# Two recurrence inverses in one pair of PSUM banks, chain products kept together, low-rank lo weights at full height

## The chip, the cores and the metric

The kernel runs on one core of a Trainium2 chip. The time is the device time of one execution in microseconds (us). A core has five engines with a queue of instructions each: TensorE (PE), which multiplies; VectorE (DVE), ScalarE (ACT) and GpSimd (POOL), which work on elements; and SyncE (SP), which issues most DMAs. Each engine takes its own instructions in order; between engines semaphores tell when data are ready. TensorE writes to PSUM, which has eight banks; a tile of 128 x 512 float32 fills one.

## The reference

One encoder layer is applied to two groups of rows (1024 and 256), 1280 in all, of width 1024. Cut to what matters here:

```python
x = x + 0.5 * rms_norm(swiglu(rms_norm(x), ...))       # first FFN
p_rw, p_att, p_gate = split(rms_norm(x) @ w_in)
y_a = rwkv7_bidir(p_rw, ...)                           # the recurrence
y_b = axial_gqa(p_att, ...)                            # attention
x = x + rms_norm((sig(gA) * (y_a @ w_branch_a) + sig(gB) * (y_b @ w_branch_b)) @ w_out)
x = x + 0.5 * rms_norm(swiglu(rms_norm(x), ...))       # second FFN

def _rwkv7_step(S, inp):                               # in rwkv7_bidir, per head and direction
    r, w, k, v, kk, b = inp
    sa = einsum('ij,j->i', S, -kk)
    S = S * w[None, :] + sa[:, None] * b[None, :] + v[:, None] * k[None, :]
    return S, einsum('ij,j->i', S, r)
```

w and a (from which k and b are made) come out of two low-rank products, `tanh(wd) @ w_up` and `ad @ a_up`, of rank 64 for each of two directions.

## The kernel before

The program is traced instruction by instruction and then scheduled: every engine's order is fixed before the run by priority, which follows the order of the trace, and by readiness. So the code's loops give the order of the work only roughly.

**Prep.** `columns` runs the big projections (L165, in `projT`) and between them, in pieces, `prep`, 20 times (4 pairs of heads q, 5 blocks of 256 rows). A piece begins with the low-rank products: for each direction d and each of w and a, one product of the weights' high half (L576, all 128 rows of the array: both directions' rows stand in `hi`, and the activations of the other direction are its low part) and one of the low half `lo` (L577), which has 64 rows, those of the direction. ACT takes tanh out of PSUM (L578), POOL scales (L580), DVE scans and multiplies (L597 to L616), and the results go to DRAM. A copy `go` of the gate product (L585) is stored by a DMA (L586). All tiles come from pools of buffers by tag; a tile that takes a buffer waits until that buffer's last reader is done.

**Recurrence.** `run` goes through 80 steps: for each q, 20 chunks of 64 rows, the forward and the backward direction of two heads together. A step has three parts. `front` (L676 to L696) multiplies a chunk's keys and queries (g), transposes, and writes Bm and Bl, the matrix that has to be inverted, high and low half in float16. `inv` (L709 to L733) inverts it: a start on POOL and DVE (L709, L711), five levels of two matmuls (L715), a mask on DVE (L717), four matmuls (L720, L721) and a copy on ACT (L723), and an end (L726 to L733) that writes TT. `chain` (L752 to L794) is what each step takes from the one before: z from the state S and the chunk (L752, L756), a copy on ACT (L759), u from TT and z (L763), two copies into UV (L764, L765), sp and yp from UV (L771, L778, L780), and the new S on DVE and POOL (L785, L786). The z, u, sp and yp products use 64 columns of the array, some of them 64 rows; the matmuls of `front` and `inv` use 128 x 128. A float32 product of this kind is two instructions in the trace.

`run` interleaves the three by ticks: four slots hold an inverse each and go on by one stage a tick; in two of a tick's four turns either a stage of `chain` or of `front` is traced, in the other two the background work `finish`. `front` may be up to seven steps ahead of `chain` (NB). In PSUM the four inverses have a bank each (`RPB["i"]`), g, z and the rest one each. `first` marks the 8 steps that have no S yet (4 q, 2 groups of rows).

Of the kernel before, what the change touches and what calls it, by code (L numbers as in the profile page):

```python
# [342 lines left out]
class Bufs:  # L343
# [5 lines left out]
    def tile(self, shape, dt, name, tag=None):  # L349
# [7 lines left out]
PQ = (4, 3)  # L357
PBT = "pb"
# [6 lines left out]
       "TT": 7, "tt": 9, "y1": 6, "zs": 2, "Sn": 3, "SP": 2}  # L365
RPB = {"i": 4, "g": 1, "z": 1, "s": 1}
# [14 lines left out]
class Rwkv:  # L381

    NB, PK, LAG, NAR, AHEAD, NI = 7, 1, 2, 8, 1, 4
# [41 lines left out]
    def prep_weights(self, q, W):  # L425
# [17 lines left out]
    def loop_consts(self, ep, cp):  # L443
# [10 lines left out]
        for i in range(self.NB):  # L454
            bm = cp.tile([128, 2, 128], F16, name=f"Bm{i}")
            bl = cp.tile([128, 2, 128], F16, name=f"Bl{i}")
# [103 lines left out]
    def prep(self, q, got, ci, W, ps):  # L560
# [10 lines left out]
        for d in range(2):  # L571
            ds_ = slice(64 * d, 64 * d + 64)
# [11 lines left out]
        o = W.tile([128, n], F32, name="go", tag="go")  # L584
# [80 lines left out]
    def front(self, pp, sd, cf, cb, W, ps, TG, res):  # L665
# [20 lines left out]
        Bm, Bl = self.Bm[self.step_no % self.NB], self.Bl[self.step_no % self.NB]  # L686
# [10 lines left out]
        TT_ = W.tile([128, 2, 128], F32, name="TT", tag="TT")  # L697
        res.update(gs=gs, BKt=BKt, UV=UV, TT=TT_, Bm=Bm, Bl=Bl)
        yield

    def inv(self, ind, W, ps, TG):

        nc = self.nc
        Bm, Bl = ind["Bm"], ind["Bl"]
        p = ps.tile([128, 4, 128], F32, name="inv", tag=TG["i"])
        m, dbl = p[:, 0:2], p.rearrange("p (h a) t -> p h a t", h=2)
        mask = lambda l: self.lv[:, l:l + 1].to_broadcast([128, 2, 128])
        tt = W.tile([128, 2, 2, 128], F16, name="tt", tag="tt")
# [4 lines left out]
        for l in range(1, 6):  # L713
            for h in range(2):
                nc.tensor.matmul(m[:, h], lhsT=Bm[:, h], rhs=tt[:, h, 0], start=True, stop=True)  # L715
            y1 = W.tile([128, 2, 128], F16, name="y1", tag="y1")
            nc.vector.tensor_tensor(out=y1, in0=m, in1=mask(l), op=ALU.mult)  # L717
            yield
            for h in range(2):
                nc.tensor.matmul(dbl[:, h, 0], lhsT=tt[:, h, 1], rhs=y1[:, h], start=True, stop=True)  # L720
                nc.tensor.matmul(dbl[:, h, 1], lhsT=y1[:, h], rhs=tt[:, h, 1], start=True, stop=True)  # L721
            tt = W.tile([128, 2, 2, 128], F16, name="tt", tag="tt")
            nc.scalar.copy(tt, dbl)  # L723
            yield
        for h in range(2):
            nc.tensor.matmul(m[:, h], lhsT=Bm[:, h], rhs=tt[:, h, 0], start=True, stop=False)  # L726
            nc.tensor.matmul(m[:, h], lhsT=Bl[:, h], rhs=tt[:, h, 0], start=False, stop=True)
        ws = W.tile([128, 2, 128], F16, name="ws", tag="y1")
        nc.vector.tensor_tensor(out=ws, in0=m, in1=tt[:, :, 0], op=ALU.subtract)
        yield  # L730
        for h in range(2):
            nc.tensor.matmul(m[:, h], lhsT=ws[:, h], rhs=tt[:, h, 1], start=True, stop=True)
        nc.vector.scalar_tensor_tensor(out=ind["TT"], in0=tt[:, :, 1], scalar=2.0, in1=m, op0=ALU.mult, op1=ALU.add)  # L733
        yield

    def chain(self, pp, sd, st, cf, cb, ind, W, ps, TG, first, early):
# [11 lines left out]
        for h in range(2):  # L748
            hs = slice(64 * h, 64 * h + 64)
            for d in range(2):  # L750
                vr = rows(1 - d)
                nc.tensor.matmul(z[rows(d), h], lhsT=gs[vr, 2 * d + h, 0:64], rhs=UV[vr, d, hs], start=h == 0, stop=first and h == 1)  # L752
        if not first:
            for h in range(2):
                for d in range(2):
                    nc.tensor.matmul(z[rows(d), h], lhsT=sd[d][0][:, cs[d] % 4, h, 0], rhs=S[:, d], start=False, stop=h == 1)  # L756
# [4 lines left out]
        for h in range(2):  # L761
            for o in (slice(0, 64), slice(64, 128)):
                nc.tensor.matmul(u[o, h], lhsT=TT_[o, h, o], rhs=zs[o, h], start=True, stop=True)  # L763
# [4 lines left out]
        for d in range(2):  # L768
            for h in range(2):
                hs = slice(64 * h, 64 * h + 64)  # L770
                nc.tensor.matmul(sp[hs, d], lhsT=BKt[:, d, hs], rhs=UV[:, d, hs], start=True, stop=True)  # L771
        yp = ps.tile([128, 2, 64], F32, name="yp", tag=TG["s"])
        for d in range(2):
            for x in range(1 if first else 2):
                for h in range(2):
                    hs = slice(64 * h, 64 * h + 64)
                    if x == 0:
                        nc.tensor.matmul(yp[hs, d], lhsT=UV[:, d, hs], rhs=gs[:, 2 * d + h, 64:128], start=True, stop=first)  # L778
                    else:
                        nc.tensor.matmul(yp[hs, d], lhsT=S[:, d], rhs=sd[d][0][:, cs[d] % 4, h, 1], start=False, stop=True)  # L780
# [7 lines left out]
        yield  # L788
# [6 lines left out]
        yield  # L795
# [39 lines left out]
    def run(self, W, ps, TG, emit):  # L835
# [22 lines left out]
        while chain_n < NS or bg:  # L858
            tick += 1
            for i in range(self.NI):  # L860
# [9 lines left out]
                if slots[i] is None and packs and packs[0][1] + self.LAG <= tick and (tick + i) % 2 == 0:  # L870
                    n, _ = packs.pop(0)
                    slots[i] = (n, self.inv(steps[n]["ind"], W, ps, TG))
                if slots[i] is not None and next(slots[i][1], 0) == 0:
                    done.add(slots[i][0])
                    slots[i] = None
# [436 lines left out]
```

## Time and profile before

| | us |
|---|---|
| median of 3 runs (3557.45 to 3557.83) | 3557.76 |
| the profiled execution's own time | 3558.98 |
| its span, from the first to the last instruction | 3557.2 |
| prep of the recurrence, within the span | 1580 to 1812 |
| recurrence (first g to last yp), within the span | 1822 to 2343 |
| granted TensorE clock, mean over the span | 0.988 |

The profile is one execution. "PE" is TensorE's matmuls, "PEld" its loads of weights, which overlap them. L165 is line 165 of the kernel. A group such as `inv<-y,tt` names the tile written and the tiles read. A matmul's end is modelled, and matmuls run pipelined, so the distance from one start to the next tells more of PE than the durations. `128*64 128x64 f32` after a matmul is rows * columns of the array, then the moving operand's shape. In the timeline, x8 merges eight instructions of a line that overlap; the time is from the first start to the last end. In brackets stands the engine's idle time before an instruction, and what ended it. In a table by stage each engine has its busy time and, in brackets, its number of instructions; after POOL come the granted clock, the DMA engines' busy share and GB/s.

### The profile page before, as it was taken

The page shows a single profiled execution, that of the slowest core. Times are in us where ns is not written, and L with a number is a line of the kernel's source. Part 1 is how long each engine was busy: PE and PEld are TensorE (multiplying, and loading weights), DVE is VectorE, ACT ScalarE, POOL GpSimd, SP SyncE. Part 2 cuts the span into 40 slices and gives each one's busy share as a digit, 9 for nine tenths or more (in the row PEclk, how much of TensorE's full clock was granted, in tenths as well). Part 3 has the DMA queues.
Part 4 walks back from the last instruction along what each step waited for, and adds up shares of the span by engine and source line. Part 5 has one row for each costly group of instructions (what it writes and reads, how often), then busy time and mean ns, then how long its engine had stood idle before and what let it go on. Part 6 is the DMA issues. An engine that isn't in the chain of part 4 may idle for free. (4 is left out here: it accounts for less than half of the span.)

```text
span 3557.2 us, 56074 instructions
## 1 busy us (share of the span) xinstructions
PE 3467.9 (97%) x22608; PEld 2907.8 (82%) x22608; DVE 1720.8 (48%) x3300; ACT 1291.6 (36%) x2524; POOL 376.7 (11%) x706
## 2 busy tenths in 40 slices
PE   8999999999899999999989999998999999999997
PEld 7888888888788888887768888888878888888886
DVE  3233333333726776648777667647332333333335
ACT  4211111111523666746556666623432111111112
POOL 0000000000301000003144444410000000000002
PEclk9999999999999999999999999999999999999999
DMA  3111111111324121224352212147221111111103
GB/s 127 42 36 36 36 48 36 42 36 35 131 83 135 59 73 45 84 77 154 130 184 85 70 54 76 41 146 236 102 83 36 42 36 36 36 45 39 36 30 119
DMA packets 155108, 264.93 MB, mean 74 GB/s; under 512 B 16864, under 2 KB 98016, under 8 KB 154720
## 3 DMA queue, kind: packets, MB, share of 16 engines
q1 hardware_dynamic: 154848, 261.34, 22.9%
q8 instruction: 178, 2.92, 0.3%
q14 instruction: 82, 0.67, 0.1%
HBM read 183.94 MB, written 74.06 MB: 73 GB/s over the span
## 5 line engine op out<-in xcount | busy, mean ns | idle before, releaser
L165 PE MATMUL pp<-hT,whi 128*128 128x512 f32 (+1 forms) x6000 | 1643.1, 360 | 7.8 <-ACT qk L950 4.9
L165 PEld LDWEIGHTS pp<-hT,whi 128*128 128x128 f32 x6000 | 1068.0, 190 | 175.6 <-ACT qk L950 5.7
L165 PE MATMUL pp<-hT,wlo 128*128 128x512 f32 (+1 forms) x3000 | 1074.4, 358 | 0.0
L165 PEld LDWEIGHTS pp<-hT,wlo 128*128 128x128 f32 x3000 | 569.3, 190 | 79.8
L141 DVE TENSOR_TENSOR wlo<-wraw,whi 128x1024 fp32r<-128x1024 f32 x125 | 154.1, 1233 | 566.7 <-ACT whi L140 566.6
L211 DVE TENSOR_TENSOR acc<-acc,pd 128x512 f32<-128x512 f32 x400 | 271.3, 685 | 203.4 <-PE pd L206 203.2
L206 PE MATMUL pd<-dh,ah 128*128 128x512 f32 x880 | 346.4, 394 | 13.8 <-DVE acc L211 13.8
L206 PE MATMUL pd<-dh,al 128*128 128x512 f32 x880 | 345.6, 393 | 0.0
L206 PE MATMUL pd<-dl,ah 128*128 128x512 f32 x880 | 345.4, 392 | 0.0
L293 POOL TENSOR_TENSOR yg<-acc,gb 128x1024 f32<-128x1024 f32 x19 | 48.2, 2544 | 2075.1 <-DMA xb<-x_d 1128.6
L723 ACT CAST tt<-inv 128x512 f16<-128x512 f32 x400 | 226.6, 588 | 90.7 <-PE inv L721 66.4
L187 DVE TENSOR_TENSOR sg<-sg,pp 128x512 f32<-128x512 f32 x132 | 79.0, 598 | 347.8 <-PE pp L165 347.8
L140 ACT CAST dh<-draw 128x1024 fp32r<-128x1024 f32 x44 | 46.0, 1046 | 528.8 <-DMA draw<-wd 528.8
L140 ACT CAST ah<-sg 128x512 fp32r<-128x512 f32 x132 | 72.2, 547 | 439.5 <-DVE sg L187 439.5
L206 PEld LDWEIGHTS pd<-dh,ah 128*128 128x128 f32 x880 | 166.7, 189 | 52.0 <-DVE acc L211 18.1
L717 DVE TENSOR_TENSOR y<-inv,lv 128x256 f16<-128x256 f32 x400 | 161.6, 418 | 83.6 <-PE inv L715 61.4
L140 ACT CAST whi<-wraw 128x1024 fp32r<-128x1024 f32 x125 | 131.1, 1049 | 194.1 <-PE pp L165 191.7
L206 PEld LDWEIGHTS pd<-dh,al 128*128 128x128 f32 x880 | 166.7, 189 | 35.3
L206 PEld LDWEIGHTS pd<-dl,ah 128*128 128x128 f32 x880 | 166.6, 189 | 33.8
L178 ACT ACTIVATE sg<-pp 128x512 f32<-128x512 f32 x132 | 69.1, 524 | 327.1 <-PE pp L165 325.8
L1156 PE MATMUL pbr<-yT,whi 128*128 128x256 f32 x640 | 124.1, 291 | 19.2 <-ACT yT L140 8.9
L720 PE MATMUL inv<-y,tt 128*128 128x128 f16 x800 | 130.7, 221 | 0.0
(228 smaller groups left out, 4868.3 us busy)
## 6 DMA issues: line engine op xcount, KB each, us to landing
wraw<-wgu SPq DMA_DIRECT2D x88, 512.0 KB, 3.5
draw<-wd SPq DMA_DIRECT2D x44, 512.0 KB, 3.8
gate_d<-go SPq DMA_DIRECT2D x16, 640.0 KB, 3.2
ar_d<-ar SPq DMA_DIRECT2D x40, 256.0 KB, 2.1
bk_d<-bk SPq DMA_DIRECT2D x40, 256.0 KB, 2.1
AR<-ar_d SPq DMA_DIRECT2D x80, 128.0 KB, 2.9
BK<-bk_d SPq DMA_DIRECT2D x40, 256.0 KB, 2.9
g<-gate_d SPq DMA_DIRECT2D x80, 128.0 KB, 3.3
```

Source lines behind the costliest of these rows:

```text
L140: self.nc.scalar.copy(dst_h, src)
L141: self.nc.vector.tensor_tensor(out=dst_l, in0=src, in1=dst_h.bitcast(F32), op=ALU.subtract)
L165: nc.tensor.matmul(p[:, :n], lhsT=a[:, ks], rhs=h[:, b, k], start=i == 0, stop=i == 23)
L178: nc.scalar.activation(out=sg[:, c0:c0 + n], in_=p[:, :n], func=AF.Silu)
L187: nc.vector.tensor_tensor(out=sg[:, s], in0=sg[:, s], in1=p[:, :n], op=ALU.mult)
L206: nc.tensor.matmul(p, lhsT=a[:, ts], rhs=b[:, hs], start=i == 0, stop=i == m - 1)
L211: nc.vector.tensor_tensor(out=acc[:, t, hs], in0=acc[:, t, hs], in1=p, op=ALU.add)
L293: (nc.vector if late else nc.gpsimd).tensor_tensor(out=yg, in0=y, in1=gbc, op=ALU.mult)
L717: nc.vector.tensor_tensor(out=y1, in0=m, in1=mask(l), op=ALU.mult)
L720: nc.tensor.matmul(dbl[:, h, 0], lhsT=tt[:, h, 1], rhs=y1[:, h], start=True, stop=True)
L723: nc.scalar.copy(tt, dbl)
L1156: nc.tensor.matmul(p, lhsT=a[:, ks], rhs=ys[ci][:, b, kk], start=i == 0, stop=i == 11)
```

## The change

- `inv` takes two steps at once: four matrices instead of two in one PSUM tile of two banks, two slots instead of four, all operations twice as wide, the same number of matmuls for a step. Bm, Bl and TT are kept by pairs of steps; a pair starts when both its fronts are done.
- `chain` traces its products in `together`: each is ordered behind the one before on PE, and all have a higher priority (300). z starts with the products of S, then those of gs; sp comes before yp, direction 1 first. Two of its stages are joined with the ones before.
- The low half of the low-rank weights gets one tile for each direction with all 128 rows, the other direction's rows cleared on POOL. The gate's copy `go` shares the buffers of tag `w1`.
- PK goes from 1 to 3; buffers of TT, tt and y1 become fewer and twice as large.

```diff
-RPB = {"i": 4, "g": 1, "z": 1, "s": 1}
+       "TT": 4, "tt": 5, "y1": 4, "zs": 2, "Sn": 3, "SP": 2}
+RPB = {"i": 2, "g": 1, "z": 1, "s": 1}
-    NB, PK, LAG, NAR, AHEAD, NI = 7, 1, 2, 8, 1, 4
+    NB, PK, LAG, NAR, AHEAD, NI = 7, 3, 2, 8, 1, 2
...
-        lo = W.tile([128, 2, 128], F32R, name="llo")
+        lo = W.tile([128, 2, 2, 128], F32R, name="llo")
         for d in range(2):
-            rs = slice(64 * d, 64 * d + 64)
-            nc.vector.tensor_tensor(out=lo[rs], in0=raw[rs, d], in1=hi.bitcast(F32)[rs, d], op=ALU.subtract)
+            rs, ot = slice(64 * d, 64 * d + 64), slice(64 - 64 * d, 128 - 64 * d)
+            nc.vector.tensor_tensor(out=lo[rs, d], in0=raw[rs, d], in1=hi.bitcast(F32)[rs, d], op=ALU.subtract)
+            nc.gpsimd.memset(lo.bitcast(F32)[ot, d], 0.0)
...
-                nc.tensor.matmul(p[:, j], lhsT=lo[ds_, j], rhs=src[ds_, d, cs], start=False, stop=True)
+                nc.tensor.matmul(p[:, j], lhsT=lo[:, d, j], rhs=src[:, d, cs], start=False, stop=True)
...
-        o = W.tile([128, n], F32, name="go", tag="go")
+        o = W.tile([128, n], F32, name="go", tag="w1")
...
+        i, j = self.step_no // 2 % len(self.Bm), self.step_no % 2
+        Bm, Bl = self.Bm[i][:, j], self.Bl[i][:, j]
+        if j == 0:
+            self.TT2 = W.tile([128, 2, 2, 128], F32, name="TT", tag="TT")
...
-        Bm, Bl = ind["Bm"], ind["Bl"]
-        p = ps.tile([128, 4, 128], F32, name="inv", tag=TG["i"])
+        Bm, Bl, TT_ = (x.rearrange("p s h t -> p (s h) t") for x in ind["pair"])
+        p = ps.tile([128, 8, 128], F32, name="inv", tag=TG["i"])
...
         for l in range(1, 6):
-            for h in range(2):
+            for h in range(4):
                 nc.tensor.matmul(m[:, h], lhsT=Bm[:, h], rhs=tt[:, h, 0], start=True, stop=True)
-            y1 = W.tile([128, 2, 128], F16, name="y1", tag="y1")
+            y1 = W.tile([128, 4, 128], F16, name="y1", tag="y1")
             nc.vector.tensor_tensor(out=y1, in0=m, in1=mask(l), op=ALU.mult)
...
+    @contextlib.contextmanager
+    def together(self):
+        tc, last = self.k.tc, []
+        def go(out, **kw):
+            with tc.issue_after(last[-1].ins) if last else contextlib.nullcontext():
+                last.append(self.nc.tensor.matmul(out, **kw))
+        with tc.high_priority(offset=CP):
+            yield go
...
+        with self.together() as go:
+            if not first:
+                for h in range(2):
+                    for d in range(2):
+                        go(z[rows(d), h], lhsT=sd[d][0][:, cs[d] % 4, h, 0], rhs=S[:, d], start=h == 0, stop=False)
             for h in range(2):
+                hs = slice(64 * h, 64 * h + 64)
                 for d in range(2):
+                    vr = rows(1 - d)
+                    go(z[rows(d), h], lhsT=gs[vr, 2 * d + h, 0:64], rhs=UV[vr, d, hs], start=first and h == 0, stop=h == 1)
...
+        with self.together() as go:
+            for h in range(2):
+                for o in (rows(0), rows(1)):
+                    go(u[o, h], lhsT=TT_[o, h, o], rhs=zs[o, h], start=True, stop=True)
...
+        with self.together() as go:
+            for d in (1, 0):
+                for hs in (rows(0), rows(1)):
+                    go(sp[hs, d], lhsT=BKt[:, d, hs], rhs=UV[:, d, hs], start=True, stop=True)
+            for d in range(2):
                 for h in range(2):
+                    go(yp[rows(h), d], lhsT=UV[:, d, rows(h)], rhs=gs[:, 2 * d + h, 64:128], start=True, stop=first)
+                if not first:
+                    for h in range(2):
+                        go(yp[rows(h), d], lhsT=S[:, d], rhs=sd[d][0][:, cs[d] % 4, h, 1], start=False, stop=True)
...
+                if i % 2 == 0:
+                    j = i // 2
+                    if slots[j] is None and len(packs) > 1 and packs[1][1] + self.LAG <= tick:
+                        n, _ = packs.pop(0)
+                        packs.pop(0)
+                        slots[j] = (n, self.inv(steps[n]["ind"], W, ps, TG))
+                    if slots[j] is not None and next(slots[j][1], 0) == 0:
+                        done.update((slots[j][0], slots[j][0] + 1))
+                        slots[j] = None
```

## Rows read from the trace of the kernel before

**Rows 1.** The page, part 1: busy us and share of span, instructions.

```profile
PE 3467.9 (97%) x22608; PEld 2907.8 (82%) x22608; DVE 1720.8 (48%) x3300; ACT 1291.6 (36%) x2524; POOL 376.7 (11%) x706
```

**Rows 2.** Table by stage: stretch, length, busy us of PE, PEld, DVE, ACT, POOL.

```profile
1600.00:1620.00 20.00, 20.00 (x104) 16.40 (x105) 19.00 (x46) 14.77 (x32) 8.35 (x15) 1.00 0.50 165
...
1580.00:1812.00 232.00, 231.63 (x1137) 180.87 (x1136) 196.88 (x457) 144.86 (x318) 62.97 (x136) 0.99 0.44 152
...
1860.00:2300.00 440.00, 436.15 (x6233) 354.24 (x6231) 307.97 (x817) 294.70 (x711) 202.80 (x421) 1.00 0.23 69
```

**Rows 3.** Timeline of PE in prep: start, us, engine, line, tiles, shapes, count.

```profile
1601.80 0.28 PE L165 MATMUL pp<-hT,whi 128*128 128x256 f32 x1
1601.92 0.28 PE L576 MATMUL pl<-low,lhi 128*128 128x256 f32 x1
1602.13 0.38 PE L577 MATMUL pl<-low,llo 64*128 64x256 f32 x1
1602.44 0.39 PE L165 MATMUL pp<-hT,whi 128*128 128x256 f32 x1
1602.66 0.28 PE L165 MATMUL pp<-hT,wlo 128*128 128x256 f32 x1
```

**Rows 4.** Timeline of PE in the recurrence.

```profile
2042.56 0.22 PE L721 MATMUL inv<-tt,y 128*128 128x128 f16 x1
2042.71 0.33 PE L752 MATMUL zu<-UV,gs 64*64 64x64 f32 x2
2042.96 0.28 PE L715 MATMUL inv<-tt,Bm 128*128 128x128 f16 x2
2043.18 0.44 PE L752 MATMUL zu<-UV,gs 64*64 64x64 f32 x6
2043.55 0.45 PE L756 MATMUL zu<-Sn,AR 128*64 128x64 f32 x8
2043.94 0.23 PE L720 MATMUL inv<-y,tt 128*128 128x128 f16 x1
```

**Rows 5.** Groups by line: count, busy us, mean ns, idle us before.

```profile
L577 PE MATMUL pl<-low,llo 64*128 64x256 f32 x80 | 30.5, 381 | 0.0
```

**Rows 6.** DMA issues: count, KB each, median us from issue to landing.

```profile
g_d<-go SPq DMA_DIRECT2D x20, 128.0 KB, 1.9
```

**Rows 7.** Timeline of PE, the last two steps' sp.

```profile
2338.56 0.27 PE L771 MATMUL sp<-UV,BKt 128*64 128x64 f32 x1
...
2342.06 0.27 PE L771 MATMUL sp<-UV,BKt 128*64 128x64 f32 x1
```

**Rows 8.** Groups by line: the inverse's operations, and two wider ones from PSUM.

```profile
L723 ACT CAST tt<-inv 128x512 f16<-128x512 f32 x400 | 226.6, 588 | 90.7 <-PE inv L721 66.4 <-POOL Bl L696 6.7 <-issue 5.9
L717 DVE TENSOR_TENSOR y<-inv,lv 128x256 f16<-128x256 f32 x400 | 161.6, 418 | 83.6 <-PE inv L715 61.4 <-ACT tt L723 13.5 <-ACT zs L759 5.0
...
L1021 ACT ACTIVATE e<-sc,nm,rq 128x1024 f32<-128x1024 f32 (+1 forms) x80 | 86.2, 1078 | 56.1 <-DVE nm L1018 53.4 <-issue 2.4
...
L683 DVE TENSOR_TENSOR gs<-g,gm 128x512 f32<-128x512 f32 x80 | 54.7, 684 | 23.5 <-PE g L676 22.5
L709 POOL TENSOR_TENSOR tt<-Bm,lv 128x256 f16<-128x256 f16 x80 | 54.3, 685 | 4.8 <-ACT UV L765 1.9 <-PE inv L721 1.5
...
L711 DVE STREAM_TRANSPOSE tt<-tt 128x256 f16<-128x256 f16 x80 | 35.1, 438 | 19.5 <-POOL tt L709 19.2
```

**Rows 9.** Timeline of POOL, PE and DVE: starts and ends of inverses.

```profile
1943.91 0.41 DVE L733 SCALAR_TENSOR_TENSOR TT<-tt,inv 128x256 f32<-128x256 f16 x1
...
1945.09 1.31 POOL L709 TENSOR_TENSOR tt<-Bm,lv 128x256 f16<-128x256 f16 x2
...
1968.13 0.41 DVE L733 SCALAR_TENSOR_TENSOR TT<-tt,inv 128x256 f32<-128x256 f16 x1
...
2337.07 0.28 PE L732 MATMUL inv<-tt,ws 128*128 128x128 f16 x2
...
2337.40 0.42 DVE L733 SCALAR_TENSOR_TENSOR TT<-tt,inv 128x256 f32<-128x256 f16 x1 [0.71 <-PE inv L732]
```

More of the change, by code (lines that the diff above doesn't have):

```diff
@@ L357 @@
 PQ = (4, 3)
+CP = 300
 PBT = "pb"
@@ L453, in loop_consts @@
         self.Bm, self.Bl = [], []
-        for i in range(self.NB):
-            bm = cp.tile([128, 2, 128], F16, name=f"Bm{i}")
-            bl = cp.tile([128, 2, 128], F16, name=f"Bl{i}")
+        for i in range((self.NB + 1) // 2):
+            bm = cp.tile([128, 2, 2, 128], F16, name=f"Bm{i}")
+            bl = cp.tile([128, 2, 2, 128], F16, name=f"Bl{i}")
             nc.gpsimd.memset(bm, 0.0)
@@ L696, in front @@
             nc.gpsimd.tensor_tensor(out=Bl[rs, :, rs], in0=src, in1=Bm[rs, :, rs], op=ALU.subtract)
-        TT_ = W.tile([128, 2, 128], F32, name="TT", tag="TT")
-        res.update(gs=gs, BKt=BKt, UV=UV, TT=TT_, Bm=Bm, Bl=Bl)
+        res.update(gs=gs, BKt=BKt, UV=UV, TT=self.TT2[:, j], pair=(self.Bm[i], self.Bl[i], self.TT2))
         yield
@@ L713, in inv @@
         for l in range(1, 6):
-            for h in range(2):
+            for h in range(4):
                 nc.tensor.matmul(m[:, h], lhsT=Bm[:, h], rhs=tt[:, h, 0], start=True, stop=True)
-            y1 = W.tile([128, 2, 128], F16, name="y1", tag="y1")
+            y1 = W.tile([128, 4, 128], F16, name="y1", tag="y1")
             nc.vector.tensor_tensor(out=y1, in0=m, in1=mask(l), op=ALU.mult)
             yield
-            for h in range(2):
+            for h in range(4):
                 nc.tensor.matmul(dbl[:, h, 0], lhsT=tt[:, h, 1], rhs=y1[:, h], start=True, stop=True)
                 nc.tensor.matmul(dbl[:, h, 1], lhsT=y1[:, h], rhs=tt[:, h, 1], start=True, stop=True)
-            tt = W.tile([128, 2, 2, 128], F16, name="tt", tag="tt")
+            tt = W.tile([128, 4, 2, 128], F16, name="tt", tag="tt")
             nc.scalar.copy(tt, dbl)
             yield
-        for h in range(2):
+        for h in range(4):
             nc.tensor.matmul(m[:, h], lhsT=Bm[:, h], rhs=tt[:, h, 0], start=True, stop=False)
             nc.tensor.matmul(m[:, h], lhsT=Bl[:, h], rhs=tt[:, h, 0], start=False, stop=True)
-        ws = W.tile([128, 2, 128], F16, name="ws", tag="y1")
+        ws = W.tile([128, 4, 128], F16, name="ws", tag="y1")
         nc.vector.tensor_tensor(out=ws, in0=m, in1=tt[:, :, 0], op=ALU.subtract)
         yield
-        for h in range(2):
+        for h in range(4):
             nc.tensor.matmul(m[:, h], lhsT=ws[:, h], rhs=tt[:, h, 1], start=True, stop=True)
-        nc.vector.scalar_tensor_tensor(out=ind["TT"], in0=tt[:, :, 1], scalar=2.0, in1=m, op0=ALU.mult, op1=ALU.add)
+        nc.vector.scalar_tensor_tensor(out=TT_, in0=tt[:, :, 1], scalar=2.0, in1=m, op0=ALU.mult, op1=ALU.add)
         yield
+    @contextlib.contextmanager
[6 more added lines that the diff above has]
+            yield go
     def chain(self, pp, sd, st, cf, cb, ind, W, ps, TG, first, early):
@@ L747, in chain @@
         rows = lambda d: slice(64 * d, 64 * d + 64)
[L748 to L753, printed above, removed]
+        with self.together() as go:
[3 more added lines that the diff above has]
+                        go(z[rows(d), h], lhsT=sd[d][0][:, cs[d] % 4, h, 0], rhs=S[:, d], start=h == 0, stop=False)
             for h in range(2):
+                hs = slice(64 * h, 64 * h + 64)
                 for d in range(2):
-                    nc.tensor.matmul(z[rows(d), h], lhsT=sd[d][0][:, cs[d] % 4, h, 0], rhs=S[:, d], start=False, stop=h == 1)
+                    vr = rows(1 - d)
+                    go(z[rows(d), h], lhsT=gs[vr, 2 * d + h, 0:64], rhs=UV[vr, d, hs], start=first and h == 0, stop=h == 1)
         pcs = PCb[:, o0:o1 + 1:o1 - o0].unsqueeze(2).to_broadcast([128, 2, 64])
@@ L787, in chain @@
         st["S"] = Sn
-        yield
         YT = pp["YT"].rearrange("p (c t) -> p c t", t=64)
@@ L859, in run @@
             tick += 1
-            for i in range(self.NI):
+            for i in range(4):
                 while pair_n < len(pairs) and pair_n <= front_n // 4 + self.AHEAD and 2 * (pair_n - chain_n // 4) < self.NAR \
@@ L869, in run @@
                     pair_n += 1
[L870 to L875, printed above, removed]
+                if i % 2 == 0:
[7 more added lines that the diff above has]
+                        slots[j] = None
                 if i in self.HP:
```

24 lines of the change are left out of this document (3 added, 21 removed).

## Prediction

> **What bounds the kernel now.** I read the page first: TensorE (PE) is busy 3467.9 us, 97% of the span [rows 1]. A busy PE is not proof of a full one, since the ends of matmuls are modelled, so next the table by stage, for the two stretches that the change touches. In the stage where the recurrence's inputs are prepared (1580 to 1812 us) PE is busy 231.6 of 232 us, and VectorE (DVE) is not far behind: 196.9 us, and in a stretch such as 1600 to 1620 it has 19.0 of 20 [rows 2]. In the recurrence (1822 to 2343 us, 80 steps; its middle stands in the table) PE is busy 436.2 of 440 us while DVE has 308.0 and ScalarE (ACT) 294.7 [rows 2]. The third view settles whether PE is full: the timeline of PE alone, read from start to start. Nearly every matmul starts when the one before lets it, and where an interval is long, it is so because the shape of the matmul changes, not because data are missing [rows 3, 4]. So PE's own order of instructions is the bound in both stages, and intervals on PE are what the change can take away. Everything else is cover.
>
> **Part 1, lo weights at full height (prep, L577).** A 256-column matmul at full height is followed 0.12 us later by the next (1601.80 to 1601.92). Around the 64-row lo product three intervals grow: into it 0.21 instead of 0.12, out of it 0.31, and the row after next comes at 0.22 instead of 0.12 [rows 3]. That is 0.09 + 0.19 + 0.10 us. There are 80 such products [rows 5]. The last of the three terms can be told for 60 of them (the other 20 are followed by the gate's two-pass product, whose own pace I can't separate). PE loses 80 x 0.28 + 60 x 0.10 = 28.4 us. At full height the added rows are zeros and the columns stay, so each lo product costs the 0.12 us of its neighbours and all 28.4 us fall away on PE. Not all can reach the end: DVE's work of 196.9 us stays, and where it fills 19.0 of 20 us only 5% can be squeezed. If 5% held for all 232 us, the gain would be 11.6 us; if DVE's 35 idle us can be used freely, 28.4. I take 20, the middle. Added are eight clears on POOL, which is the least busy engine (63 of 232 us) [rows 2], so nothing. The gate's copy "go" now shares three buffers with the scans: it holds one until its store has landed, 1.9 us [rows 6], and a later ScalarE write (L601) may stand in front of that, with the exponentials behind it. ACT has 87 of 232 us free [rows 2], which hides it; without the cover it is 20 x 1.9 = 38 us at worst. I take 0 to 4, within the low end.
>
> Full-height rows follow at 0.12 us though each brings its own weights [rows 3], so their loads run under the matmul before. [...]
>
> **Part 2, unbroken chain groups (L752 to L780).** The chain's products use a part of the array. From an inverse's full matmul to such a product PE takes 0.15 us (2042.56 to 2042.71) against 0.06 between two inverse matmuls (a pair of them lasts 0.28, one 0.22); out again, the last of a group of eight starts 0.22 us before the group's end, at 2043.78, and the inverse follows at 2043.94: 0.16 against 0.03 in the group [rows 4]. So a group that is broken once more costs 0.09 + 0.13 = 0.22 us. The row pattern shows one: two of the eight z products, two inverse matmuls, then the other six [rows 4]. Over the stage I count 324 unbroken runs of chain products on PE's timeline; three groups a step for 80 steps would be 240. 84 x 0.22 = 18.5 us, all on PE. The change inside the z group from one tile shape to another stays.
>
> Two new waits come with it. The z group now starts with the products of S, so the gs products, which were ready earlier, stand behind POOL's Sn; then the sp products stand ahead of yp and wait for the second copy of UV. Both lengthen the chain's own path by about 0.4 us (eight products of 0.03 and a switch of 0.15), and inverse matmuls stand behind them on PE. At the end, with little else to do, steps follow at 3.50 us [rows 7]; with 0.4 more it is 3.9, well below the 6 us that PE needs for a step. So nothing is taken for it.
>
> **Part 3, two inverses in one pair of banks.** The matmuls are the same in number and size. DVE and ACT save fixed cost, which is worth nothing as neither bounds. What changes is how many inverses are in flight: four singles become two pairs. Unloaded, a level of a single inverse takes 0.28 (two matmuls: 0.06 and 0.22 to the end) + 0.42 (DVE) + 0.40 (four) + 0.59 (ACT) + four hand-overs of 0.1 = 2.09 us; five levels, 1.3 at the start (POOL 0.69, DVE 0.44, two hand-overs) and 1.8 at the end (0.40, 0.28 and twice 0.41) make 13.6 [rows 8]. The hand-over is an estimate: 0.05 from PE to DVE (2337.35 to 2337.40) [rows 9], and more back to PE. Of a pair, the tile operations on 128x512 and 128x1024 from PSUM are not in the trace for this line; I take those of the same shapes, 0.684 (L683) and 1.078 (L1021); they can't be under the single's 0.42 and 0.59, nor over twice these [rows 8]. A level is then 0.40 + 0.68 + 0.64 + 1.08 + 0.4 = 3.20, the end 2.7, the start 2.4 (both single rows doubled), together 21.1 us; with the two ends, 16.8 and 22.7.
>
> Now the room. Four steps take 24.2 us (TT at 1943.91 and 1968.13), and an inverse's own time in that, from POOL's first operation to TT's end, is 1945.09 to 1968.54, 23.4 us [rows 9]: 9.8 us of it are waits, which cost nothing as four run at once and PE is full. After the change PE needs 24.2 - 84/20 x 0.22 = 23.3 us for four steps. A pair has a slot for that long. Its start doesn't touch the banks and can run under the pair before, so 18.7 us + waits must fit. Each meets one other pair instead of three other inverses, with larger operations; I take half of the waits, 4.9 us, so 23.6 us for four steps, 0.6 less than now. Times 20 that is -12 us: of the 18.5 of part 2 some 6 are given back.
>
> Fill and drain: the first pair is ready 21.1 - 13.6 = 7.5 us later, two steps at once; later, two chains are left at the end. Between 0 and 11 (7.5 and one step of 3.5 [rows 7]); I take 6.
>
> **The sum.** -20 - 12 + 6 = -26 us. The profiled execution took 3558.98 us, 1.2 above the median of 3557.76; so 3532 for the median.
>
> **Rivals.**
> *A*, the above: 3532. Prep lies between -11.6 and -28.4, the recurrence between -18.5 and 0, the fill between 0 and 11; with all three at one end it is 3511 or 3557. As they won't all fall together, its own range is 3515 to 3549.
> *B*, the other side: the pairs become the bound of the recurrence. If they wait 7.8 us, four fifths of today's, four steps take 18.7 + 7.8 = 26.5 us, 2.3 more than now: +46. 3557.8 - 20 + 46 + 6 = 3590. It decides from 24.9 us for four steps, where 14 us of loss and 6 of fill eat prep's 20. For it: an unloaded pair fills 21.1 of 23.3 us. Against it: a third of the competitors, and room under the pair before.
> *C*, the unbroken groups don't pay: put at the head of PE's queue, a group waits for ACT's copy or POOL's Sn with inverse matmuls ready behind it, 0.23 us a step or more, and runs are merged for nothing. With 24.2 to 24.9 us for four steps: 3544 to 3558; I put it at 3555, no change.
> *D*, prep doesn't pay in full because DVE is full there: a gain of 11.6 less the 4 of "go", 7.6 instead of 20: 3544. For it: 19.0 of 20 us [rows 2].
> *E*, a load shown for each full-height lo product, 80 x 0.19 = 15 us (the 0.31 less 0.12 of today's lo row [rows 3]): 3547. [...]
>
> **How the numbers follow.** Chances: A 0.53, B 0.21, C 0.15, D 0.09, E 0.02. About 0.2% (7 us) is what a measurement of this kernel can tell from no change. A, D and E are faster by more: 0.64; C is the same: 0.15; B slower: 0.21. The range takes in A's, C and the near part of B: 3510 to 3578; above it lies rather more than half of B, below it a full prep gain with nothing given back.
>
> **What would show it.** In the trace after: L577 as 128-row products, 0.12 us apart from their neighbours, and prep shorter by some 20 us with DVE above 90% (right); prep as long as now with PE idle (D). Some 240 runs of chain products and 0.15 us at each edge (part 2). For part 3, TT twice as wide every 11.8 us or so: 23.6 us for two pairs means A; 25 or more, with PE idle before L715 and L720 and ACT or DVE named as what ended it, means B. Idle PE before the z or u products names C. The prediction is wrong altogether if something outside these two stages moves by more than some us, since no line of it is touched.

## The result, and the profile after

The change makes the kernel slower: 3663.3 us (3660.1 to 3666.2) against 3557.7 on the same chip, a ratio of 1.0298 (95% interval 1.0284 to 1.0313). The profiled execution has a span of 3658.1 us. I read it in the order of [rows 1 and 2].

The page's part 1 of the kernel after (busy us, share of the span, instructions), and under it the groups by line of the two evictions of a pair (count, busy us, mean ns, idle us before and who ended it):

```profile
PE 3468.4 (95%) x22608; PEld 2902.8 (79%) x22608; DVE 1699.9 (46%) x2980; ACT 1264.7 (35%) x2324; POOL 380.0 (10%) x668
...
L728 ACT CAST tt<-inv 128x1024 f16<-128x1024 f32 x200 | 199.5, 1013 | 104.1 <-PE inv L726 89.0
...
L722 DVE TENSOR_TENSOR y<-inv,lv 128x512 f16<-128x512 f32 x200 | 136.6, 689 | 106.6 <-PE inv L720 98.3
```

PE's sum of busy time is that of the kernel before, and the span is 101 us longer. But the sum hides two opposite changes: in prep PE is busy 19 us less, and in the recurrence (first g to last sp) 26 us more, 538.4 us where it was 512.2, with 82 us of the recurrence at a granted clock of 0.50 where it was 8 (the records of the clock in the two traces hold 1.00 and 0.50 alone). The larger part of the loss is waiting: PE is idle for 93.1 us of the recurrence where it was for 7.9. ACT's 128x1024 eviction took 1013 ns where the estimate was 1078 [rows 8], and DVE's 128x512 one 689 where it was 684, so no operation came out notably dearer than taken. The table by stage of the kernel after (columns as in [rows 2]):

```profile
1600.00:1620.00 20.00, 19.21 (x97) 15.16 (x97) 19.86 (x47) 13.61 (x29) 6.22 (x14) 1.00 0.59 201
1620.00:1640.00 20.00, 19.82 (x121) 16.61 (x121) 14.29 (x32) 9.98 (x20) 0.78 (x10) 1.00 0.25 80
...
1810.00:1820.00 10.00, 5.49 (x19) 4.04 (x20) 4.23 (x5) 1.79 (x3) 8.51 (x15) 0.56 0.95 272
...
1580.00:1812.00 232.00, 212.33 (x1133) 171.25 (x1131) 200.48 (x463) 143.37 (x316) 71.86 (x147) 0.97 0.47 161
1860.00:2300.00 440.00, 382.98 (x5197) 302.63 (x5196) 234.52 (x440) 219.69 (x434) 162.93 (x321) 0.93 0.21 62
```

In prep PE now has room (212 of 232 us). DVE is full where its work is densest (19.86 of 20 us in 1600 to 1620), but not throughout: in 1620 to 1640 PE is the fuller one, and in the last 10 us neither is, while POOL (8.51 us) and the DMA engines (0.95) are the busiest. In the recurrence PE is busy 383 of 440 us where it had 436 [rows 2]. The recurrence's first g product starts at 1815.67 instead of 1822.42 us, so prep gained 6.7 us; from there to the last sp it is 631.2 us instead of 519.9. The whole loss is the recurrence, and PE's waits in 1780 to 2480 name who ended them (us in total, times, longest):

```profile
PE inv L720 <- ACT tt L728: 29.7, 63, 1.2
PE inv L725 <- DVE y L722: 14.3, 41, 0.8
PE zu L748 <- POOL Sn L803: 11.6, 32, 1.6
PE inv L731 <- ACT tt L728: 10.9, 21, 0.7
PE inv L737 <- DVE ws L734: 7.5, 19, 0.9
```

PE stands before the inverses' own products and waits for the two evictions: what was priced as hidden is in the open. How the waits lie in time is plainest in a table of four adjoining stretches of the kernel after:

```profile
1942.00:1958.00 16.00, 14.17 (x235) 11.25 (x237) 8.58 (x17) 5.89 (x15) 8.77 (x17) 1.00 0.16 48
1958.00:1972.00 14.00, 10.09 (x139) 7.82 (x135) 6.62 (x12) 7.95 (x11) 2.15 (x5) 1.00 0.15 43
1972.00:1988.00 16.00, 14.99 (x225) 11.75 (x223) 8.48 (x17) 5.98 (x15) 8.76 (x17) 0.89 0.16 46
1988.00:2002.00 14.00, 11.64 (x146) 9.37 (x142) 8.81 (x17) 9.08 (x15) 2.15 (x5) 1.00 0.16 45
```

For 16 us four chain steps and the fronts that they release keep PE busy for 89 and 94%; then for 14 us there is little but the two pairs, and PE is idle for up to 28% of the time. The kernel before has 16.00, 13.95, 15.98 and 13.97 us of PE in the same four stretches. The intervals from one step's sp to the next go by fours, such as 5.5, 6.1, 4.4, 14.4 us (before: 7.1, 5.8, 6.9, 4.5). In the slack stretch the two pairs go in step and meet at ACT, as ACT's timeline shows (a row "x2" is two evictions back to back):

```profile
1963.16 1.93 ACT L728 CAST tt<-inv 128x1024 f16<-128x1024 f32 x2 [1.56 <-PE inv L726]
1966.11 1.93 ACT L728 CAST tt<-inv 128x1024 f16<-128x1024 f32 x2 [1.02 <-PE inv L726]
```

From 1963.16 to 1966.11 is one level of both pairs, 2.95 us. And in one of the two places a pair starts late. DVE's last operation of a pair, then POOL's timeline up to the start of the next in that place:

```profile
1940.22 0.69 DVE L738 SCALAR_TENSOR_TENSOR TT<-tt,inv 128x512 f32<-128x512 f16 x1 [0.49 <-PE inv L737]
...
1942.97 0.40 POOL L803 TENSOR_TENSOR Sn<-Sn,pc 128x128 f32<-128x128 f32 x1 [8.41 <-DVE Sn L802]
1943.66 0.97 POOL L698 TENSOR_TENSOR Bm<-gs,e 64x128 f16<-64x128 f32 x2 [0.28 <-DVE gs L685]
1944.71 0.92 POOL L702 TENSOR_TENSOR Bl<-gs,Bm 64x128 f16<-64x128 f32 x2
1945.71 1.16 POOL L714 TENSOR_TENSOR tt<-Bm,lv 128x512 f16<-128x512 f16 x1
```

The next pair's two fronts had their gs at 1918.9 and 1925.3 and their last Bl at 1928.1, 17.6 us before, yet its start at 1945.71 stands on POOL's queue behind Sn, and behind Bm and Bl of a step seven ahead, which waited for the chain (8.41 us of idle).

In the other place the next start, at 1950.52, lies 0.8 us ahead of the end of the pair before; there the second front is late, with its Bl at 1945.6. Over the starts from 1900 to 2300 us a pair is in flight 29.8 us on average, from POOL's start to TT's end, and the next start in its place follows 1.0 us behind.

### The profile page after: what moved, and what is told of

It is laid out like the page before. It is cut to its first block, busy times and chain, and to the rows that moved or that the text cites. A ratio compares the mean times of both kernels' runs of the same rounds, so it can differ in the third digit from the quotient of the medians.

```text
span 3658.1 us, 55075 instructions
## 1 busy us (share of the span) xinstructions
PE 3468.4 (95%) x22608; PEld 2902.8 (79%) x22608; DVE 1699.9 (46%) x2980; ACT 1264.7 (35%) x2324; POOL 380.0 (10%) x668
## 5 line engine op out<-in xcount | busy, mean ns | idle before, releaser
L728 ACT CAST tt<-inv 128x1024 f16<-128x1024 f32 x200 | 199.5, 1013 | 104.1 <-PE inv L726 89.0
L722 DVE TENSOR_TENSOR y<-inv,lv 128x512 f16<-128x512 f32 x200 | 136.6, 689 | 106.6 <-PE inv L720 98.3
L725 PE MATMUL inv<-y,tt 128*128 128x128 f16 x800 | 122.2, 224 | 14.6 <-DVE y L722 14.3
```

## The experiments

All runs in one table. "Four steps" is the time from the first to the last sp of the recurrence in the trace, over 79, times 4. The difference is to the kernel before on the same chip, and runs are compared by it.

| run | what it is | us | difference | ratio (95%) | four steps |
|---|---|---|---|---|---|
| before | | 3557.7 | | 1 | 25.0 |
| after | lo, groups, pairs | 3663.3 | +105.6 | 1.0298 (1.0284 to 1.0313) | 30.1 |
| e1_lo | before + lo | 3550.1 | -4.3 | 0.9987 (0.9978 to 0.9996) | 25.0 |
| e2_chain | before + groups | 3574.1 | +19.7 | 1.0057 (1.0044 to 1.0071) | 25.9 |
| e3_pair | before + pairs | 3588.2 | +33.8 | 1.0096 (1.0083 to 1.0110) | 26.4 |
| e4_lo_chain | before + lo + groups | 3565.6 | +11.2 | 1.0030 (1.0018 to 1.0041) | 25.8 |
| e5_after_short | after, a level less | 3606.0 | +51.6 | 1.0139 (1.0124 to 1.0154) | 27.5 |
| e6_before_short | before, a level less | 3543.0 | -11.4 | 0.9963 (0.9948 to 0.9978) | 24.3 |
| e7_after_early | after, pair's start in the front | 3641.3 | +86.9 | 1.0246 (1.0231 to 1.0261) | 29.1 |
| e9_after_nopri | after, no priority | 3608.3 | +53.9 | 1.0153 (1.0136 to 1.0170) | 27.3 |
| e10_chain_nopri | e2, no priority | 3586.6 | +30.4 | 1.0089 (1.0074 to 1.0104) | 26.5 |
| e11_after_noorder | after, priority without the tie | 3655.6 | +99.4 | 1.0283 (1.0268 to 1.0299) | 29.8 |
| e15_nopri_nb8 | e9, ring of eight steps | 3610.1 | +53.9 | 1.0150 (1.0133 to 1.0167) | 27.5 |
| e16_nopri_split | e9, ACT eviction split with DVE | 3664.9 | +108.7 | 1.0308 (1.0293 to 1.0323) | 30.3 |
| e18_chain_zb | e10, z group as before | 3572.0 | +17.5 | 1.0049 (1.0034 to 1.0065) | 25.8 |
| e19_best | e18 + lo + turns as before | 3546.8 | -7.7 | 0.9979 (0.9971 to 0.9988) | 24.7 |
| e20_pair_zb | e9, z group as before | 3597.4 | +42.8 | 1.0119 (1.0105 to 1.0132) | 26.9 |
| e21_pair_best | e19 with pairs | 3586.1 | +31.3 | 1.0088 (1.0070 to 1.0107) | 26.3 |
| e22_turns | before, two turns fewer | 3565.1 | +10.3 | 1.0027 (1.0017 to 1.0036) | 25.6 |

**One part at a time.** Each takes its part of the diff into the kernel before, nothing else:

```diff
e1: + lo = W.tile([128, 2, 2, 128], ...)   lhsT=lo[:, d, j]   "go" on tag w1
e2: + CP = 300, together(), chain() of after (z order, sp before yp, two yields fewer)
e3: + inv() on pairs, NI = 2, PK = 3, buffers of after
```

> The kernel before with part 1 alone: full-height lo weights, and the gate's copy in the buffers of w1. If VectorE fills prep once PE's 28 us are gone (theory: prep is bound by VectorE), the time falls by 4 to 10 us, about as far as prep shrank in the changed kernel (the recurrence's first product at 1815.7 instead of 1822.4). If PE were the only bound it would fall by 20 to 28.

> The kernel before with part 2 alone: chain products kept together at high priority, four single inverses. Theory L (the pair's latency made the loss): PE stays the bound and some 84 broken runs are merged, so the time falls by 10 to 18 us. Theory G (unbroken groups at the head of PE's queue wait, with ready inverse products behind them): it rises by 20 to 110 us.

> The kernel before with part 3 alone: two inverses in one pair of banks, two slots; chain and low-rank weights as before. Theory L: the whole loss is here, +90 to +130 us, and each TT is used within some 2 us of its being written. Theory G: no loss, between -15 and +10 us.

> The kernel before with parts 1 and 2, without the pairs. Theory L: the gains of the two add, -15 to -28 us, faster than both kernels (3530 to 3543). Theory G: slower than before by 10 to 100 us.

e1 gains 4 us and no more, as expected if DVE fills prep. Its row 1600 to 1620 of the table by stage shows DVE with 20.00 of 20. What sets the end of prep, where neither PE nor DVE is full, was not separated.

```profile
1600.00:1620.00 20.00, 19.24 (x99) 15.06 (x99) 20.00 (x48) 14.12 (x30) 6.18 (x14) 1.00 0.60 198
```

e2 loses 20 where the expectation of theory L had a gain. e3 loses 34 (it takes PK, the two places and the buffers along, so this is the price of all of them), and its trace gives the pair's length. DVE's and POOL's timeline of e3, end of one pair, start and end of the next, start of the third in the same place:

```profile
1931.95 0.69 DVE L737 SCALAR_TENSOR_TENSOR TT<-tt,inv 128x512 f32<-128x512 f16 x1 [0.20 <-PE inv L736]
...
1932.49 1.16 POOL L713 TENSOR_TENSOR tt<-Bm,lv 128x512 f16<-128x512 f16 x1
...
1958.26 0.69 DVE L737 SCALAR_TENSOR_TENSOR TT<-tt,inv 128x512 f32<-128x512 f16 x1 [0.20 <-PE inv L736]
...
1958.80 1.16 POOL L713 TENSOR_TENSOR tt<-Bm,lv 128x512 f16<-128x512 f16 x1
```

A pair has its place from 1932.49 to 1958.95, 26.5 us, and the next start lies 26.3 us behind the last: a pair's own length is the pace. Over the starts from 1900 to 2300 us a pair is in flight 26.5 us on average, and the next start follows 0.8 us behind its end. The parts alone come to -4 + 20 + 34 = +50, together to +106; e4 shows that lo and groups add up to within 5 us (-4 + 20 = 16 for 11). So groups and pairs do something to each other that neither does alone.

**Does the pair's length set the pace?** One level of five left out, after and before:

```diff
-        for l in range(1, 6):
+        for l in range(1, 5):
```

> The changed kernel with the last of the five levels of every inverse left out (so that work is missing: per pair 12 products, one DVE eviction, one ACT eviction; the rest is unchanged). Theory L (a pair's own length sets the recurrence: two places, each taken 28 to 30 us for two steps): a level is 0.69 us on DVE, 1.01 us on ACT, its products of about 1.4 us and the waits between them, some 3.6 us of a pair's length; with two places at work for 40 pairs that is 20 times 3.6 = 72 us less, so 3663 falls to about 3575 to 3600. Theory P (TensorE's own work sets it): only the products are gained, 40 pairs by 12 products of about 58 ns = 28 us, so about 3635.

> The kernel before with the last of the five levels of every inverse left out (that work is missing: per step 6 products, one DVE and one ACT eviction). Four single inverses run at once and TensorE is 99% busy in the recurrence. If products bound it (theory P): 80 steps by 6 products of 58 ns = 28 us and a few of the smaller waits, so 3520 to 3532. If the length of an inverse set it already before (theory L for the kernel before): a level is about 2.3 us of 13.6 us unloaded and more under load, 80 by 2.3 over 4 places = 46 us or more, so under 3512.

After gets 54 us shorter, twice what the products left out are worth (28): 54 over the 20 turns of each place is 2.7 us, near a level's own length in the rows above (2.95). Before gives back only 11. There PE is full in the table by stage, 437.38 of 440 us:

```profile
1860.00:2300.00 440.00, 437.38 (x5982) 345.90 (x5982) 296.64 (x768) 260.79 (x652) 210.49 (x433) 1.00 0.24 71
```

480 products at 57 ns from start to start are 27 us less; the changes of tile shape on PE rise from 722 to 815, and 93 by the 0.15 us of [rows 4] are, as an estimate, 14 more; 13 remain. So the recurrence before is bound by PE, and after in the main by its pairs.

**What the groups do to the pairs.** The priority left out of the kernel after, then the priority kept and the tie left out:

```diff
e9:
-        with tc.high_priority(offset=CP):
-            yield go
+        yield go
e11:
-            with tc.issue_after(last[-1].ins) if last else contextlib.nullcontext():
+            with contextlib.nullcontext():
```

> The changed kernel without the priority of 300 for the chain's groups (the with-line that raises it is left out); the products of a group are still issued one behind the other, and nothing else differs. Theory I (alone the three parts cost -4, +20 and +34 us, together +105: the missing 55 us come from the raised priority, which puts the chain's products early in TensorE's queue, so that the chain goes in bursts of four steps and the pairs wait behind them): the sum of the parts comes back, 3600 to 3612, and the intervals between state updates become even. Theory L (a pair's length and its two places, whatever the order of the chain): within 15 us of 3663, with a long interval once in four steps as now.

> The changed kernel with the raised priority kept, but without the tie that issues a group's products one behind the other; nothing else differs. Theory I (the raised priority alone makes the 55 us that the parts do not add up to): within 12 us of 3663. If the tie makes them: 3600 to 3620, as without the priority.

Without the priority 52 of the 106 us are back, with it and without the tie 6. So it is the priority. It is also the priority, not the tie, that keeps the chain's products together on PE: they stand there in 239 runs after, in 240 without the tie (e11), in 268 without the priority (e9). e9's first two stretches of the same table are the fuller ones, 15.8 of 16 and 12.3 of 14 us where after had 14.2 and 10.1, and so is a longer one, 322 of 350 us where after has 304:

```profile
1942.00:1958.00 16.00, 15.80 (x239) 12.83 (x240) 9.24 (x18) 9.84 (x19) 6.79 (x15) 1.00 0.20 61
1958.00:1972.00 14.00, 12.32 (x174) 10.04 (x171) 7.91 (x16) 5.92 (x12) 5.38 (x10) 1.00 0.28 84
...
1900.00:2250.00 350.00, 322.26 (x4619) 261.91 (x4613) 212.75 (x401) 196.18 (x383) 144.71 (x284) 0.99 0.23 66
```

A pair is in flight as long in e9 as in after (30.0 and 29.8 us on average); what differs is the next start, 2.2 us ahead of the end in e9 and 1.0 behind it in after.

Without priority the parts do add up: -4 (e1) + 30 (e10) + 34 (e3) = 60 for 54. The start of a pair moved forward in POOL's and DVE's queues:

```diff
 front(), second step of a pair, behind Bl:
+            nc.gpsimd.tensor_tensor(out=tt[:, :, 1], in0=Bm pair, in1=lv[:, 0:1], op=ALU.mult)
+            nc.vector.transpose(tt[:, :, 0], tt[:, :, 1])
```

> The changed kernel, with the start of a pair (the product with the first mask on POOL and its transpose on DVE) issued in the front of the pair's second step, right behind that step's Bl, and one more buffer for its result; nothing is left out. Theory Q (a pair that follows another in its place starts 4.5 to 6 us late, as its start stands on POOL's queue behind the Sn, Bm and Bl of a later step, whose products wait for the chain): one of the two places loses about 5 us for every pair, 20 pairs by 5 = 100 us at most where one place alone sets the pace and half of it where both do, so 3663 falls by 40 to 60 us to about 3605 to 3620. Theory L (the length of a pair alone): the start takes 2.4 us of it, of which the early issue takes away 20 by 2.4 = 48 us at most; then the gaps behind a pair stay as they are. Theory I (the unbroken groups, placed early in TensorE's queue, hold up everything else): within 10 us of 3663.

It gives 19 us, not 40 to 60, and even these can't be put down to the start alone: in the recurrence PE is idle as long as in after (93.2 and 93.1 us), and what falls is its busy time (518.8 for 538.4), at a granted clock of 0.50 for 35 us instead of 82. What starts earlier is in flight longer: 37 us on average over the starts from 1900 to 2300, where after has 30. How the 52 us of the priority split among the queues and the clock wasn't separated. Two more runs ask what limits the pairs in e9, the ring of buffers or the evictions:

```diff
e15: NB = 8, gs/BKt/UV 8 buffers, y1 2
e16:
-            nc.scalar.copy(tt, dbl)
+            nc.scalar.copy(tt[:, 0:2], dbl[:, 0:2])
+            nc.vector.tensor_copy(tt[:, 2:4], dbl[:, 2:4])
```

> The changed kernel without the raised priority (3608), with the fronts allowed eight steps ahead of the chain in place of seven and eight buffers of gs, BKt and UV in place of seven (y1 from four to two to make room). Theory L (two places, each taken 27 us by a pair, bound the recurrence: behind one pair's TT the next starts at once): within 6 us of 3608. Rival N (the ring of seven steps bounds it, since a pair needs the front of its second step and so has only six steps of room: chain step to gs 1 us, to the start 3 to 8, the pair 27 to 30, to the state update 2 to 6, some 37 to 41 us for six steps of 6.7 = 40 us): the start comes sooner and each six steps take some 3 us less, 13 by 3 = 40 us, so 3570 to 3585.

> The changed kernel without the raised priority (3608), with each ACT eviction of a pair (1.01 us for 128x1024) split in two halves, one on ACT and one on DVE, at once. Theory L (the length of a pair sets the pace, 26.9 us for four steps in each place): a level gets shorter by 1.01 - 0.6 = 0.4 us, a pair by five times that, 2 us, so 20 rounds of the two places give 40 us: 3565 to 3580. Rival (DVE, 60% busy in this stretch, takes 100 halves a place of about 0.69 us more and makes the y evictions late by as much as the halves gain): 3600 to 3625.

A longer ring makes no difference (53.9 us to before in both), unless the two buffers of y1 that it lost took back a gain. The split eviction should have shortened a level and costs 55 us more than e9. PE's waits in e16, 1815 to 2460 us, name DVE, whose queue now holds both evictions of every level (the first of the two lines stands at 6.9 us in e9):

```profile
PE inv L725 <- DVE y L722: 20.7, 46, 0.8
PE inv L720 <- DVE tt L729: 14.0, 21, 2.0
```

Shorter operations on paper are no shorter pair when each stands in a longer queue: a pair is in flight 32.8 us on average, where e9 has 30.0. The queue need not be all of it: in the recurrence PE's idle time rises by 22 us against e9 (58.2 to 80.6) and its busy time by 36 (516.9 to 553.3), with 88 us at a granted clock of 0.50 instead of 29.

**Why the groups cost by themselves.**

> The kernel before with the chain's groups of the changed one (order of the products, unbroken, two turns of the planner fewer per step) and single inverses, but without the raised priority; it is the earlier run of the groups alone (3574, +20) less its priority. Theory I (the early place in TensorE's queue costs, the unbroken order does not): the 84 runs fewer are kept, 84 by 0.22 = 18 us at most, and the waits of the group on POOL's Sn (11.4 us) go: 3540 to 3560. If the groups cost by their own order, whatever their place (rival C of the prediction): 3568 or more.

> Single inverses, the chain's groups of the changed kernel without priority (3587), but the z group in the order of before and untied: the four products of gs first, those of the state S last, so that other products may stand between them. Theory W (the unbroken z group stands at the head of TensorE's queue and waits for POOL's Sn, 28 waits of 28.4 us in all; the old order fills that time with the products of gs): these waits go, at most 80 more switches of 0.15 us come back, so 3555 to 3572. Rival T (two turns of the planner fewer per step, or the unbroken sp and yp products, shift the whole order): 3580 or more.

> The kernel before with only the two turns at the end of a chain step left out (no other change). Theory W in its wider form (what matters is how many other products stand in TensorE's queue between a state update and the z group that waits for it, and the turns put them there): the z products of gs wait for DVE's Sn and those of S for POOL's, as in the run with the old z order and the fewer turns (12.1 and 6.1 us of waits), so 3568 to 3580. Rival (the turns matter only together with the unbroken groups): 3552 to 3560.

e18 puts the z group back (products of gs first, untied); e22 takes only two turns of the planner out of the kernel before:

```diff
 e22, chain():
         st["S"] = Sn
-        yield
 ...
             nc.vector.tensor_tensor(out=dst, in0=dst, in1=yp, op=ALU.add)
-        yield
```

The priority isn't what costs with single inverses: without it the groups lose more, 30 instead of 20. But without it they hardly stay groups: the chain's products stand in 307 runs in e10, in 259 in e2, in 324 before. PE's waits of e10, and of e18, over 1815 to 2460 us, and e22's:

```profile
PE zu L744 <- POOL Sn L798: 28.4, 28, 1.6
```

```profile
PE zu L763 <- DVE Sn L796: 12.1, 11, 1.1
PE zu L767 <- POOL Sn L797: 6.1, 12, 1.0
```

```profile
PE zu L756 <- POOL Sn L786: 12.4, 29, 1.0
```

One such wait on PE's timeline of e10:

```profile
1963.56 0.22 PE L722 MATMUL inv<-tt,y 128*128 128x128 f16 x1
1965.35 0.45 PE L744 MATMUL zu<-Sn,AR 128*64 128x64 f32 x8 [1.57 <-POOL Sn L798]
1965.73 0.45 PE L744 MATMUL zu<-UV,gs 64*64 64x64 f32 x8
1966.11 0.40 PE L716 MATMUL inv<-tt,Bm 128*128 128x128 f16 x4
```

PE stands for 1.57 us at the head of its queue; ACT's copies of tt had ended by 1964.55, but the L716 products behind the z group run at 1966.11. With the old z order the waits for POOL are a fifth, z now waits for DVE's Sn instead, less often, and 13 us are back. With the turns alone left out and all else as before, z already comes too near behind the state it waits for, 12.4 us in 29 waits where before had 0.8 in one: +10.

**Both ways put together.**

> The changed kernel without priority (3608) and with the z group in the order of before, untied. Theory W for the 18 us by which this stands above the pairs alone less the low-rank part (3588 - 4 = 3584): the waits for POOL's Sn (10.2 us, 25) go and the chain gets shorter, 3585 to 3600. Theory L (a pair's length in its place sets the pace, 26.9 us for four steps, the chain has slack): within 6 us of 3608.

> The kernel before with the low-rank part of the changed one, the unbroken u and sp/yp groups without priority, the z group as before and the five turns of the planner per step as before. Theory W: only what waits for nothing is unbroken, so the runs fewer (some 40 of 84, by 0.22 us = 9 us) are pure gain on top of the 4 us of the low-rank part: 3538 to 3548, below both kernels. Rival T (if the turns are the cause, they show here against e18): with the turns back and the z order back nothing is lost either, but if e18 is 3580 or more and this one near 3550, the turns were it. If the unbroken sp and yp products cost by themselves: over 3556.

> Pairs of inverses, with everything else as in the version that came to 3547 (low-rank part, unbroken u and sp/yp groups without priority, z group and turns of before). Theory L (two places, each taken 26 us by a pair): the pairs alone lost 34 us and lose as much here, 3572 to 3588, with about 26 us for four steps. Rival (pairs lost only by the way the groups stood): below 3547, as their 160 switches fewer would give.

e20 gains 11 us over e9: with pairs, too, part of the groups' loss is that wait (10.2 us in 25 waits for POOL's Sn in e9, 1.5 in 3 for DVE's in e20). e19 keeps the lo weights and the tied u and sp/yp groups, with the z order and the turns of before: 3546.8, below both kernels (0.9979, 0.9971 to 0.9988), and no wait of z is left among PE's larger ones. Whether the ties add anything to e1's gain isn't shown: the intervals of the two overlap, and e19's chain products stand in 334 runs, where before has 324. e21 differs from it by the pairs alone, and they cost 39 us there. Pairs lose whatever the groups do.

## Why the prediction was wrong, step by step

**What bounds the kernel.** Right: e6 shows PE's own order as the bound of the recurrence before. It was read as if PE would stay the bound, and it didn't.

**Part 1.** The cost on PE was right. PE's timeline of the kernel after, against [rows 3]:

```profile
1601.82 0.28 PE L579 MATMUL pl<-low,llo 128*128 128x256 f32 x1
1601.94 0.39 PE L165 MATMUL pp<-hT,wlo 128*128 128x512 f32 x1
```

The lo product is followed at 0.12 us like its neighbours, so rival E, with 0.19 us of load to show for each, is out: the lo product's load, 0.19 us from 1601.70, begins under the matmul before (L578, 0.38 us from 1601.60), and that of the product behind it, 0.19 us from 1601.82, under the lo product. The step that failed is "I take 20, the middle". The end got 6.7 us (4.3 alone), less than the low bound of 11.6 and near rival D's 7.6. Some of the 6.7 may be scatter: over all profiles the recurrence's first g lies at 1820.3 us on average with the old lo weights (seven runs) and at 1815.6 with the new (twelve), 4.7 us earlier. The low bound took DVE's 5% of room as a mean over the stage; in 1600 to 1620 DVE went from 19.00 [rows 2] to 19.86, and that was all there was in the dense stretches; in others PE stayed the fuller engine.

**Part 2.** The count was right: 239 runs of chain products after, 240 expected, and 160 changes of tile shape fewer on PE (562 for 722). But it is right in the sum only: taken by group, the kernel before has 156 runs of z, 85 of u and 86 of sp and yp for its 80 steps (some touch, so they come to 324), the kernel after 90, 83 and 102. So what there was to merge was the z group, the very one that waits. The step that failed is "nothing is taken for it", the new waits. It compared a mean, 3.9 us of chain with 6 us of PE's work; the wait comes from the place in the queue, and e10 measures 28.4 us in 28 waits for POOL's Sn (e2, with the priority, 11.4 in 19). Two edits had no price at all: the two turns of the planner that chain() no longer takes (10 us, e22), and the priority (52 us beside pairs; with single inverses it gains 11, e2 against e10).

**Part 3.** With pairs alone (e3) the waits of a pair were nearly right: 26.5 us in its place less the 21.1 worked out unloaded is 5.4, where 4.9 was taken. In the kernel after they were not: 29.8 less 21.1 is 8.7. The step that failed is "its start ... can run under the pair before": in e3 the next start lies 0.15 us ahead of the end in the rows above and 0.8 behind it on average, where the prediction has it 2.4 ahead. The planner gives a place away only when a pair's last turn is over, and POOL takes the start behind a later step's Bm and Bl. So four steps need 26.4 us (e3), not 23.6, and PE waits. A hidden start alone would not have saved the sum: in e9 the next start does lie 2.2 us ahead of the end, but a pair is in flight 30.0 us, and four steps take 27.3. Fill: the first sp comes 37.1 us behind the first g where it was 27.1, 10 us for the 6 taken (7 in e3), within its bounds.

**The rivals.** B named the mechanism, pairs that bound the recurrence; that its 26.5 us for four steps meet e3's 26.4 is luck in the terms, for B has 18.7 and 7.8 us of waits and e3 21.1 and 5.4. C named the wait at the head of PE's queue, D the full DVE. They were weighed as if one alone could come true. All three did, D in part of prep, and none held the loss that groups with priority and pairs make together, so the range ended at 3578.

## What to carry to other kernels

When an engine is 99% busy because four chains of work are in flight, halving their number and doubling their size takes away its cover: work out how long one item keeps its place, from start to next start, with the start counted in unless the queue order shows that it can move up, and compare that with the time that the full engine needs. A group put early and unbroken into an in-order queue is priced by what stands behind it while it waits (28.4 us in 28 waits in e10), not by its own length; and count first which group is broken at all, for here it was the one that waits. Price every line of a diff, priorities and planner turns too, and when several rivals touch different stages or parts, add them.

## What the hardware showed that was not expected

In the recurrence the granted clock of PE fell in some stretches, to a mean of 0.89 in 1972 to 1988 us: it stood at 0.50 from 1972.3 to 1975.7, 3.4 of the 16 us, and at 1.00 for the rest. Ahead of it PE had been busy only 10.09 of 14 us; whether that lowered the clock was not shown. It is not what makes most of the loss: e11 differs from after by the tie, its clock over 1900 to 2250 us is 0.99 (after 0.94), and it is 6 us nearer to before, not 106. But it is a part of it. e7's four runs are one program, and they go from 3639.7 us at a mean clock of 0.986 to 3650.2 at 0.978: 10.5 us for some 59 us more at 0.50 (an estimate: twice the share that the mean lacks, times the time, if these runs too stand at 1.00 or 0.50 alone). At that rate, as an estimate, the 74 us by which after's recurrence spends longer at 0.50 than before's (82 and 8) are some 13 of the 106 us. The differences between after and e7, after and e9, and e9 and e16 hold such a part too.
